# The mixer's output projection in matmuls of 256 columns instead of 512, on one core of a Trainium2

## The chip, the cores and the metric

The kernel runs on one core of a Trainium2 chip. The metric is the device time of one execution in microseconds, as the median of several runs. A core has a tensor engine (PE; its loads of stationary operands are listed on their own as PEld), a vector engine (DVE), a scalar engine (ACT), GpSimd (POOL), and a sync engine (SP) whose queue issues the DMA transfers here.

## The reference

Two layers over 256 tokens of width 1024 in float32. Each layer has three sub-layers, each with an RMS norm ahead of it and behind it:

```python
for l in range(DEPTH):
    h = _swiglu(_rmsnorm(x, g[0]), ffn_w_in[l, 0], ffn_w_out[l, 0])
    x = x + 0.5 * _rmsnorm(h, g[1])
    h = _mixer(_rmsnorm(x, g[2]), mix_w_in[l], mix_w_out[l], ...)
    x = x + _rmsnorm(h, g[3])
    h = _swiglu(_rmsnorm(x, g[4]), ffn_w_in[l, 1], ffn_w_out[l, 1])
    x = x + 0.5 * _rmsnorm(h, g[5])
```

The mixer projects the tokens to 3080 columns, runs four heads of differential attention and four heads of an mLSTM on them, and joins the two results of 512 columns each to `y`, 256 x 1024. Its last step is the output projection `y @ w_out` with a weight matrix of 1024 x 1024. This step is the one that is changed, once in each layer.

## The kernel before

The 256 tokens are two tiles of 128. A product with a weight matrix is made by `mm3` (lines 328 to 332) in three passes of float32r: each operand is split into a hi and a lo part, and hi*hi (L330), hi*lo (L331) and lo*hi (L332) add up in one PSUM bank of 128 x 512 float32. The transposed activations, 128 x 128, are the stationary operand, and the weights move, 512 columns to a matmul. The first two passes share the stationary operand `xh`, the third has `xl`.

The weights come in pieces of 1 MiB by a DMA on SP's queue (L265). ACT makes the hi part of a piece's half (`wh`, L280) and DVE the lo part (`wl`, L282). The tiles for these parts are few, so a cast often waits until PE has finished with an earlier piece.

The program's order is: feed-forward, mixer, feed-forward, for each of the two layers. In the mixer, `traverse` runs the input projection with the attention and the mLSTM between its products. Then comes the output projection (lines 615 to 638). It takes four pieces of weights and four banks `po[t][hf]` (named `bk` in the profile), one for each token tile t and half hf of the columns. `outp(t, part, hf)` makes four contraction steps k of three passes each into such a bank; part 0 is the attention's half of `y`, part 1 the mLSTM's. There are eight calls of `outp` in a layer, so 32 products or 96 matmuls. `outputs_ml` puts four transposes (L773) between them, and the next phase's `prenorm` eight transposes (L349). When a token tile's two banks are done, `postnorm` (lines 386 to 400) reads them: a square on ACT (L392) and a product on DVE (L395).

An order of instructions is set in two ways. From a phase's "ending" to the next feed-forward's "running" the order on PE is that of the program text, and this holds for the whole mixer. Elsewhere on PE, and on the other engines everywhere, a planner orders the instructions by readiness under its own costs, with a few turns given by hand (`after`).

Of the kernel before, what the change touches and what calls it, by code (L numbers as in the profile page):

```python
"""Two layers of macaron FFN / (diff attention | mLSTM) mixer / macaron FFN on one core.

Every product with a weight matrix runs as three float32r passes: an operand is
split exactly into hi (float32r, 12 significant bits) and lo = value - hi, and
hi*hi + hi*lo + lo*hi accumulate in one PSUM bank. The activations (transposed,
128 tokens a tile) are stationary and the weights move, 512 columns at a time.
"""
# [15 lines left out]
P = 128  # L23
# [26 lines left out]
def _pack(inp):  # L50
    """Lays the inputs out for the kernel, in the order in which it uses them."""
# [67 lines left out]
class _Trunk:  # L119
# [49 lines left out]
    def constants_mix(self):  # L169
# [26 lines left out]
        # lambda of both layers, on every partition  # L196
# [8 lines left out]
        # persistent tiles with fixed parts  # L205
# [25 lines left out]
    def after(self, ins, others):  # L231
        """ins takes its turn on its engine behind the others."""
        for o in others:
            self.tc.add_manual_dep(ins.ins, o.ins.name, mybir.DependencyInfo(
                mybir.DependencyClass.NoSync, mybir.DependencyReason.DATA), reason="turn")

    def table(self, name, last=None):
        """Loads a set of ScalarE's functions behind everything that uses another set."""
        self.loaded = self.nc.scalar.preload_act_table_set(name)
        self.after(self.loaded, self.users + ([last] if last else []))  # L240
        self.users = []

    def func(self, *args, **kw):
        """An activation that needs the set loaded last."""
        i = self.nc.scalar.activation(*args, **kw)  # L245
        self.after(i, [self.loaded])
        self.users.append(i)
        return i

    def piece(self):  # L250
        """The next 1 MiB of the weights as hi and lo: two times [P, 1024] each. While no
        mixer needs them, its 4 KiB buffers hold some of these."""
        parts = self.begin_piece()
        return [parts(), parts()]

    def begin_piece(self):
        """A function that gives a piece's halves one after the other."""
        nc, i = self.nc, self.piece_at
        self.piece_at += 1
        step = 1024  # L260
        if i in self.early:
            raw, step = self.early[i], 512
        else:
            raw = self.raw_tile(i)
            self.load = nc.sync.dma_start(raw.rearrange("p a b -> p (a b)"), self.a["w"][i])  # L265
        js = iter(range(2))

        def part():
            j = next(js)
            if self.lend and self.halves % 10 in (2, 5, 8):  # L270
                lo = self.k4.tile([P, 1024], F32R, tag="k4", name=f"wl_{i}_{j}")
                hi = self.k4.tile([P, 1024], F32R, tag="k4", name=f"wh_{i}_{j}")
            else:
                lo = self.wl.tile([P, 1024], F32R, tag="wl", name=f"wl_{i}_{j}")
                hi = self.wh.tile([P, 1024], F32R, tag="wh", name=f"wh_{i}_{j}")
            self.halves += 1
            turns = self.turns.pop(0) if self.turns else ()
            for c in range(0, 1024, step):
                cs = slice(c, c + step)
                ia = nc.scalar.activation(hi[:, cs], raw[:, j, cs], AF.Copy)  # L280
                self.cast = ia
                iv = nc.vector.tensor_tensor(lo[:, cs], raw[:, j, cs], hi[:, cs].bitcast(F32), op=ALU.subtract)  # L282
                for oa, ov in turns:
                    self.after(ia, [oa] if oa else [])
                    self.after(iv, [ov] if ov else [])
            return hi, lo

        return part
# [4 lines left out]
    def start(self):  # L293
        """The first loads, in the order in which the products need them."""
# [20 lines left out]
    def warm(self, n):  # L315
        """The tensor engine's clock rises while it waits for the first loads."""
        bank = self.bank_bk()
        for _ in range(n):
            self.nc.tensor.matmul(bank, self.zero[:, 0:P], self.zero, start=True, stop=True)

    @staticmethod
    def cols(piece, k):
        """Columns k*512..k*512+511 of a piece, hi and lo."""
# [4 lines left out]
    def mm3(self, ps, xh, xl, wh, wl, start, stop):  # L328
        mm = self.nc.tensor.matmul
        mm(ps, xh, wh, start=start, stop=False)  # L330
        mm(ps, xh, wl, start=False, stop=False)  # L331
        mm(ps, xl, wh, start=False, stop=stop)  # L332

# [1 line left out]
    def rsqrt(self, ss, width=1):  # L335
        """ss -> ss ** -0.5 on [P, width]."""
# [4 lines left out]
    def prenorm(self, t, gi):  # L341
        """Transposed x * gain of token tile t as hi/lo."""
        return [self.prenorm_half(t, gi, hf) for hf in range(2)]
# [19 lines left out]
    def square(self, t, hf, ss):  # L363
        """The mean square of half of token tile t."""
# [3 lines left out]
    def rstd(self, t):  # L368
        """rsqrt(mean(x ** 2) + eps) of token tile t."""
# [5 lines left out]
    def rsqrt_sum(self, ss, eps):  # L375
        """(ss0 + ss1 + eps) ** -0.5"""
# [9 lines left out]
    def postnorm(self, t, po, g, half):  # L386
        """x += (0.5 if half else 1) * rmsnorm(po) * g."""
# [83 lines left out]
    def ffn(self, pre, gi_post):  # L471
# [16 lines left out]
        if not xT:  # L488
            # the first phase: both token tiles from the start
# [41 lines left out]
        else:  # L531
            # the first two chunks: the first token tile runs ahead of the second
# [46 lines left out]
        # the last chunks: all of the first token tile, then the second  # L579
# [15 lines left out]
    def mixer(self, pre, gi_post):  # L595
# [19 lines left out]
        # output projection  # L615
# [4 lines left out]
        def outp(t, part, hf):  # L620
            for k in range(4):
                yh, yl = m.yT[t][part]
                self.mm3(po[t][hf], yh[:, k, :], yl[:, k, :], *self.cols(ws[2 * part + k // 2], 2 * (k % 2) + hf),
                         start=part == 0 and k == 0, stop=part == 1 and k == 3)
# [15 lines left out]
    def lambdas(self):  # L640
        """-(exp(q1.k1) - exp(q2.k2) + lambda_init) of both layers, on every partition."""
# [8 lines left out]
class _Mixer:  # L650
    """The stages of one layer's mixer, in the order in which they are traced."""
# [13 lines left out]
    def traverse(self, tr, pin, ws, pins1, ws1, load_gpost):  # L665
        """The rest of the input projection in steps of three matrix products, with everything
        else that the mixer does between them."""
# [53 lines left out]
    def stages(self):  # L721
        """(step, stage): the stage takes its turn once so many steps of the products are traced."""
# [37 lines left out]
    def part(self, t, kh, pin, w):  # L760
        """Half the contraction of one token tile with one group of 512 columns."""
# [7 lines left out]
    def transposed(self, a, tag="ptr"):  # L769
        """The four 128-column blocks of a, transposed, in a PSUM bank."""  # L770
# [12 lines left out]
    # ---- queries and keys of the mLSTM  # L783
# [31 lines left out]
    # ---- gates of the mLSTM  # L815
# [13 lines left out]
    def gate_inputs(self):  # L829
        """log i and the forget gate's input, tokens on partitions."""  # L830
# [24 lines left out]
    def gate_rows(self):  # L855
        """Cumulative log forget gates b, u = log i - b and the running maxima, heads on
        partitions 0..3, 32..35, 64..67 and 96..99."""
# [34 lines left out]
    def gate_exps(self, t):  # L892
        """exp(u_s - M_j) within a chunk and s <= j, zero elsewhere: one contraction over both."""
# [9 lines left out]
    def gate_decays(self):  # L903
        """The decays, input weights and exp(-m)."""
# [8 lines left out]
        # the first chunk's state is zero: its queries meet it with a factor of zero  # L913
# [5 lines left out]
    def weighted_qk(self):  # L919
        """Queries times their decay, keys times their input weight."""  # L920
# [24 lines left out]
    def intra_weights(self):  # L945
        """exp(u_s - M_j) * (k_s . q_j) / 8. Heads on other partitions use another PSUM bank."""
# [13 lines left out]
    # ---- attention  # L960
# [15 lines left out]
    def roped(self, i, t, scale):  # L976
        """Queries (i = 0) or keys (i = 1), transposed."""
# [10 lines left out]
    def scores(self, t, h0):  # L988
        """Both softmaxes of some heads before the division: exp(s - max) and its sums."""
# [29 lines left out]
    def combine(self, t, h0):  # L1019
        """l0 * (p0 - lambda * p1), transposed: [key, head, query]."""  # L1020
# [37 lines left out]
    # ---- state and output of the mLSTM; column 128 of a head's values is one, for the denominator  # L1058
# [36 lines left out]
    def output_gate(self, pin, t):  # L1095
        """tanh(o / 2): sigmoid(o) is half of it plus one."""
# [9 lines left out]
    def normed_ml(self, t):  # L1106
        """rmsnorm(num / max(|den|, exp(-m))) but for its gain: the norm takes the division's place."""
# [18 lines left out]
    def outputs_ml(self, t):  # L1126
        """sigmoid(o) times the normed output, transposed."""
# [37 lines left out]
```

## Time and profile before

| | |
|---|---|
| median of 3 runs | 1016.41 us (1015.97 to 1016.7) |
| span of the profiled execution | 1012.0 us |
| PE busy in it | 997.7 us (99%), 4701 matmuls, 4701 loads |
| DVE, ACT busy | 616.0 us (61%), 523.5 us (52%) |
| mean granted clock of PE | 0.997 |
| moved by DMA | 178.86 MB |

The span reaches from the first to the last instruction of the profiled execution; the timed runs also hold what lies around it. Busy time of PE is the union of its matmuls, each listed with its full latency, so matmuls in a row overlap; what one of them takes of the engine's time is read from the distance between two starts. Shapes are given as rows*columns of the stationary operand, then partitions x elements of the moving one. The type float32r is listed as f32 for PE.

### The profile page before, as it was taken

To read this page: it belongs to the slowest core of one execution; us is meant where nothing else is said; L and a number is where in the kernel's file an instruction comes from. 1 tells how busy PE (TensorE), PEld (TensorE's weight loads), DVE (VectorE), ACT (ScalarE), POOL (GpSimd) and SP (SyncE) were. 2 spreads that over 40 slices of the span, in tenths; PEclk is the share of its full clock that TensorE was granted. 3 is DMA by queue.
4 is the path that set the end of the run, shared out by engine and by line. 5 is a ranking of instruction groups with operands and counts; after the bars stand their busy time and mean duration, and the time that the engine had idled before them with its cause. 6 is when DMAs were issued, how large, how long until landed. Compare 5 with 4: busy or idle time off the path is not lost.

```text
span 1012.0 us, 12195 instructions
## 1 busy us (share of the span) xinstructions
PE 997.7 (99%) x4701; PEld 807.3 (80%) x4701; DVE 616.0 (61%) x867; ACT 523.5 (52%) x853; POOL 58.3 (6%) x60
## 2 busy tenths in 40 slices
PE   8999999999999999999999999999999999999997
PEld 5888888887788888888888888888877888888885
DVE  6755454589766755555485545456988586454542
ACT  6644444466755654444375544445768465444431
POOL 2000000014010000000000000001230100000000
PEclk9999999999999999999999999999999999999999
DMA  7954545335352745454346455543554247554511
GB/s 276 353 206 151 197 172 191 131 125 186 132 202 84 279 158 208 166 214 191 136 177 260 152 188 201 191 148 119 179 176 140 110 163 274 185 190 166 206 45 42
DMA packets 26809, 178.86 MB, mean 177 GB/s; under 512 B 2970, under 2 KB 3354, under 8 KB 6014
## 3 DMA queue, kind: packets, MB, share of 16 engines
q1 hardware_dynamic: 26750, 178.07, 48.4%
q8 instruction: 37, 0.61, 0.2%
q14 instruction: 22, 0.18, 0.1%
HBM read 177.01 MB, written 1.05 MB: 176 GB/s over the span
## 4 chain that ended last, share of the span: by engine, by line
PE 92%; DVE 5%; ACT 1%; DMA 1%; issue 0%; SPq 0%; DVEq 0%; POOLq 0%; ACTq 0%
PE pin L330 19%; PE pin L332 18%; PE pin L331 18%; PE bk L330 10%; PE bk L332 10%; PE bk L331 10%; PE ptr L461 2%; DVE wl L282 2%; DVE conv L806 1%; PE ptr L349 1%; PE ptr L773 1%; DMA wr<-in_w_dram 1%; ACT p L245 1%; PE bk L1086 1%; PE bk L1041 1%; ACT wh L280 0%
## 5 line engine op out<-in xcount | busy, mean ns | idle before, releaser
L282 DVE TENSOR_TENSOR wl<-wr,wh 128x1024 fp32r<-128x1024 f32 (+1 forms) x332 | 397.6, 1219 | 229.2 <-ACT wh L280 225.8
L280 ACT ACTIVATE wh<-wr 128x1024 fp32r<-128x1024 f32 (+1 forms) x332 | 340.4, 1045 | 203.5 <-PE pin L332 110.9
L330 PE MATMUL pin<-wh,th 128*128 128x512 f32 x880 | 350.7, 399 | 0.6 <-DVE rb L972 0.6
L332 PE MATMUL pin<-wh,tl 128*128 128x512 f32 x880 | 344.8, 392 | 0.0
L331 PE MATMUL pin<-wl,th 128*128 128x512 f32 x880 | 344.7, 392 | 0.0
L332 PEld LDWEIGHTS pin<-wh,tl 128*128 128x128 f32 x880 | 165.2, 188 | 36.4
L330 PEld LDWEIGHTS pin<-wh,th 128*128 128x128 f32 x880 | 165.3, 188 | 35.8 <-issue 1.0
L331 PEld LDWEIGHTS pin<-wl,th 128*128 128x128 f32 x880 | 165.5, 188 | 33.3
L330 PE MATMUL bk<-wh,hh 128*128 128x512 f32 x352 | 141.5, 402 | 0.0
L331 PE MATMUL bk<-wl,hh 128*128 128x512 f32 x352 | 139.6, 396 | 0.0
L332 PE MATMUL bk<-wh,hl 128*128 128x512 f32 x352 | 139.3, 397 | 0.0
L464 ACT ACTIVATE hh<-ptr 128x256 fp32r<-128x256 f32 x88 | 33.2, 378 | 101.2 <-PE ptr L461 83.3
L245 ACT ACTIVATE sil<-pin,rs 128x256 f32<-128x256 f32 x86 | 40.7, 473 | 75.3 <-PE pin L332 70.6
L332 PEld LDWEIGHTS bk<-wh,hl 128*128 128x128 f32 x352 | 66.2, 188 | 15.2
L331 PEld LDWEIGHTS bk<-wl,hh 128*128 128x128 f32 x352 | 66.2, 188 | 14.4
L330 PEld LDWEIGHTS bk<-wh,hh 128*128 128x128 f32 x352 | 66.2, 188 | 14.5
L465 DVE TENSOR_TENSOR hl<-ptr,hh 128x256 fp32r<-128x256 f32 x88 | 37.1, 422 | 59.2 <-ACT hh L464 56.3
L454 DVE SCALAR_TENSOR_TENSOR h<-pin,rs,sil 128x256 f32<-128x256 f32 x86 | 41.3, 480 | 31.9 <-ACT sil L245 31.9
L338 POOL TENSOR_TENSOR rs<-s,c_half 128x1 f32<-128x1 f32 x24 | 18.3, 766 | 623.1 <-DVE s L378 613.3
L461 PEld LDWEIGHTS ptr<-c,h 128*128 128x128 f32 x176 | 24.6, 140 | 11.9
L395 DVE TENSOR_TENSOR tmp<-bk,gpost 128x512 f32<-128x512 f32 x24 | 16.3, 689 | 29.3 <-ACT junk L392 29.3
L461 PE MATMUL ptr<-c,h 128*128 128x128 f32 x176 | 33.5, 272 | 0.0
(169 smaller groups left out, 617.0 us busy)
## 6 DMA issues: line engine op xcount, KB each, us to landing
wr<-in_w_dram SPq DMA_DIRECT2D x162, 1024.0 KB, 4.8
gpost<-in_gpost_dram SPq DMA_DIRECT2D x6, 512.0 KB, 6.4
wr<-in_w_dram SPq DMA_DIRECT2D x3, 512.0 KB, 8.9
x<-in_x_dram SPq DMA_DIRECT2D x4, 256.0 KB, 7.0
out_dram<-x SPq DMA_DIRECT2D x4, 256.0 KB, 2.0
wr<-in_w_dram SPq DMA_DIRECT2D x2, 256.0 KB, 4.6
lamv<-in_lam_dram SPq DMA_DIRECT2D x1, 256.0 KB, 3.2
c<-in_c_dram SPq DMA_DIRECT2D x1, 222.0 KB, 6.7
```

Source lines behind the costliest of these rows:

```text
L245: i = self.nc.scalar.activation(*args, **kw)
L280: ia = nc.scalar.activation(hi[:, cs], raw[:, j, cs], AF.Copy)
L282: iv = nc.vector.tensor_tensor(lo[:, cs], raw[:, j, cs], hi[:, cs].bitcast(F32), op=ALU.subtract)
L330: mm(ps, xh, wh, start=start, stop=False)
L331: mm(ps, xh, wl, start=False, stop=False)
L332: mm(ps, xl, wh, start=False, stop=stop)
L338: self.nc.gpsimd.tensor_tensor(r, ss, self.half[:, :width], op=ALU.pow)
L395: nc.vector.tensor_tensor(tmp[hf], po[hf], g[:, hf * 512:hf * 512 + 512], op=ALU.mult)
L454: nc.vector.scalar_tensor_tensor(h, pin[:, 256:512], r, sil, op0=ALU.mult, op1=ALU.mult)
L461: nc.tensor.transpose(ptr[:, k, :], h[:, k * P:(k + 1) * P], self.ident)
L464: nc.scalar.activation(hh, ptr, AF.Copy)
L465: nc.vector.tensor_tensor(hl, ptr, hh.bitcast(F32), op=ALU.subtract)
```

## The change

`mm3` passes further keywords on to the matmuls. In the mixer's output projection each product of 512 columns becomes two of 256 columns, into the first and the second half of the same bank. Each of the two makes its three passes with the same stationary operands. The flag that starts a bank's sum is set on the first half of the first product alone, and the flag that ends it on both halves of the last. The products of the feed-forward and of the mixer's input projection stay as they are. The rest of the diff only blanks comments and docstrings, and is left out here; the line numbers up to the output projection stay the same.

```diff
-    def mm3(self, ps, xh, xl, wh, wl, start, stop):
+    def mm3(self, ps, xh, xl, wh, wl, start, stop, **kw):
         mm = self.nc.tensor.matmul
-        mm(ps, xh, wh, start=start, stop=False)
-        mm(ps, xh, wl, start=False, stop=False)
-        mm(ps, xl, wh, start=False, stop=stop)
+        mm(ps, xh, wh, start=start, stop=False, **kw)
+        mm(ps, xh, wl, start=False, stop=False, **kw)
+        mm(ps, xl, wh, start=False, stop=stop, **kw)
...
         def outp(t, part, hf):
             for k in range(4):
                 yh, yl = m.yT[t][part]
-                self.mm3(po[t][hf], yh[:, k, :], yl[:, k, :], *self.cols(ws[2 * part + k // 2], 2 * (k % 2) + hf),
-                         start=part == 0 and k == 0, stop=part == 1 and k == 3)
+                wh, wl = self.cols(ws[2 * part + k // 2], 2 * (k % 2) + hf)
+                for n in range(2):
+                    c = slice(n * 256, n * 256 + 256)
+                    self.mm3(po[t][hf][:, c], yh[:, k, :], yl[:, k, :], wh[:, c], wl[:, c],
+                             start=part == 0 and k == 0 and n == 0, stop=part == 1 and k == 3, skip_group_check=True)
```

## Rows read from the trace of the kernel before

**Rows 1.** The page: busy time, granted clock by slice, chain that ended last.

```profile
PE 997.7 (99%) x4701; PEld 807.3 (80%) x4701; DVE 616.0 (61%) x867; ACT 523.5 (52%) x853; POOL 58.3 (6%) x60
...
PEclk9999999999999999999999999999999999999999
...
PE 92%; DVE 5%; ACT 1%; DMA 1%; issue 0%; SPq 0%; DVEq 0%; POOLq 0%; ACTq 0%
```

**Rows 2.** All waits of PE: total us, times, longest us.

```profile
PE bk L330 <- ACT th L358: 2.9, 1, 2.9
PE bk L924 <- DVE eh L917: 1.5, 2, 0.8
PE bk L319 <- DVE mp L875: 1.2, 1, 1.2
PE ptr L773 <- POOL ra L973: 0.9, 2, 0.5
PE pin L330 <- DVE rb L972: 0.6, 2, 0.3
PE bk L1088 <- DVE C L1074: 0.4, 2, 0.2
```

**Rows 3.** Windows on the two output projections; the columns stand in the first line.

```profile
core 0: us, PE busy (x) PEld busy (x) DVE busy (x) ACT busy (x) POOL busy (x), PEclk, DMA share, GB/s
295.50:319.00 23.50, 23.50 (x114) 19.35 (x112) 13.95 (x19) 9.48 (x16) 0.55 (x1) 1.00 0.37 135
...
792.00:816.50 24.50, 24.50 (x119) 20.32 (x118) 15.02 (x21) 9.96 (x17) 0.55 (x1) 1.00 0.37 129
```

**Rows 4.** Tiles yh and bk: count, min/median/max ns, first and last start us.

```profile
L330 PEld LDWEIGHTS bk<-wh,yh x64: 187/188/190, 295.5 to 815.7; 128*128 128x128 f32 x64
...
L331 PE MATMUL bk<-wl,yh x64: 387/389/398, 295.8 to 816.2; 128*128 128x512 f32 x64
...
L332 PE MATMUL bk<-wh,yl x64: 387/391/397, 296.1 to 816.4; 128*128 128x512 f32 x64
...
L1041 PE MATMUL bk<-vd,aT x48: 270/275/275, 282.1 to 781.9; 128*128 128x128 f32 x48
```

**Rows 5.** Timeline of PE in the first output projection: start us, duration us, instruction.

```profile
299.01 0.39 PE L331 MATMUL bk<-wl,yh 128*128 128x512 f32 x1
...
304.09 0.40 PE L332 MATMUL bk<-wh,yl 128*128 128x512 f32 x1
...
308.01 0.39 PE L332 MATMUL bk<-wh,yl 128*128 128x512 f32 x1
...
312.79 0.39 PE L332 MATMUL bk<-wh,yl 128*128 128x512 f32 x1
```

**Rows 6.** Timeline of PE and its loads behind a break, products of the mixer's input.

```profile
260.57 0.19 PEld L330 LDWEIGHTS pin<-wh,th 128*128 128x128 f32 x1
260.57 0.50 PE L330 MATMUL pin<-wh,th 128*128 128x512 f32 x1
260.68 0.19 PEld L331 LDWEIGHTS pin<-wl,th 128*128 128x128 f32 x1
...
260.91 0.39 PE L331 MATMUL pin<-wl,th 128*128 128x512 f32 x1
260.91 0.19 PEld L332 LDWEIGHTS pin<-wh,tl 128*128 128x128 f32 x1
```

**Rows 7.** Timelines: the second load and second matmul of L924's pair.

```profile
245.53 0.19 PEld L924 LDWEIGHTS bk<-eh,c_hotp 36*128 36x128 f32 x1
...
245.64 0.28 PE L924 MATMUL bk<-eh,c_hotp 36*128 36x256 f32 x1
```

**Rows 8.** Timeline of PE: first and last of 16 gate products in a row.

```profile
206.38 0.22 PE L822 MATMUL bk<-th,c_wgc 128*16 128x128 f32 x1
...
207.27 0.23 PE L823 MATMUL bk<-tl,c_wgc 128*16 128x128 f32 x1
```

**Rows 9.** Timeline of PE: the attention's 24 matmuls with the values, merged.

```profile
282.07 2.84 PE L1041 MATMUL bk<-vd,aT 128*128 128x128 f32 x24
```

**Rows 10.** Timeline of ACT and DVE where the first output projection ends.

```profile
316.39 1.04 ACT L280 ACTIVATE wh<-wr 128x1024 fp32r<-128x1024 f32 x1
...
317.47 1.23 DVE L282 TENSOR_TENSOR wl<-wr,wh 128x1024 fp32r<-128x1024 f32 x1 [0.25 <-ACT wh L280]
...
319.71 0.60 ACT L392 ACTIVATE junk<-bk 128x512 bf16<-128x512 f32 x1 [1.70 <-PE bk L332]
```

## What I expect, and why

> **What bounds the kernel now.** I read the page's first two parts, then the waits of PE, then the two stretches in which the change lies, and last the single instructions in them. The page [rows 1]: PE is busy 997.7 us of a span of 1012.0, its granted clock stands in the top tenth in every slice, and 92% of the chain that ended last lies on PE. The waits of PE [rows 2]: the longest is 2.9 us, for the first operand at the beginning, and the other five kinds come to 4.6 us in all, so no other engine holds PE up for more than a few us over the whole run. The stages [rows 3]: the first output projection starts at 295.5 us and the second has its last matmul at 816.4 [rows 4]; the two windows are theirs. In both PE is busy for the whole of the window (23.50 of 23.50, 24.50 of 24.50) at a granted clock of 1.00, its upper level of 2.4 GHz, while ACT is busy for 9.48 and DVE for 13.95 us of the first. So whatever PE needs more or less there reaches the end one for one, and what the other engines do there has room.
>
> Of the stage's products the trace has 64 of each of the three passes [rows 4]: 192 matmuls of 512 columns, and as many loads of the stationary operand, one for each matmul. The median of some 390 ns for a matmul is a latency and not its price, as the next one starts long before it ends; the price is the distance from start to start [rows 5]. From 299.01 to 304.09 us lie 22 steps, 230.9 ns each; from 308.01 to 312.79 us 21 steps, 227.6 ns each. I take the mean, 229.3 ns. At 2.4 GHz 512 columns alone are 213.3 ns, so 16.0 ns of each step are something else. The question of this change is whether those 16.0 ns belong to an instruction, and are then paid twice, or grow with the columns, and are then halved.
>
> **The change part by part.** *Removed:* 192 matmuls of 512 columns with 192 loads, at 229.3 ns: 44.03 us. *Added:* 384 matmuls of 256 columns with 384 loads. The same columns stream, the same sums are made in the same four banks. The order of the program puts the three passes of the first 256 columns ahead of the three of the second.
>
> The trace of before has no float32r matmul of 256 columns and 128 rows in a row of such, so its step is bounded from both sides.
>
> - The load. After a break, two loads stand 0.11 us apart (260.57 and 260.68), and the second matmul starts 0.23 us after its load [rows 6]: a load occupies its path for about 0.11 us. In steady running it starts with the matmul ahead of it (260.91 both), so 0.11 us of load lies under 0.23 us of streaming and costs nothing. With 256 columns (106.7 ns) the cover is just as long as the load. That is the point where the change could become dear, and the nearest row for it is L1041 [rows 9]: 24 matmuls with loads of the same 128x128 size within 2.84 us, the last one 0.275 us long as the median is [rows 4], so (2.84 - 0.275) / 23 = 111.5 ns a step. There too every load lies under only one such step, and a load that were not covered would add its own 0.11 us. So a load of this size can follow every 111.5 ns, and 111.5 ns is the lower bound.
> - The step from two sizes of the same type. The gate products L822 and L823 are float32r matmuls of 128 columns and 128 rows [rows 8]: 15 steps from 206.38 to 207.27 us, 59.3 ns each. A line through 59.3 ns at 128 and 229.3 ns at 512 columns rises by 0.4427 ns a column and gives 116.0 ns at 256. Their load is of 16 columns only, so this row says nothing of the cover; L1041 does.
> - A look at 256 columns itself: L924 is float32r with 256 columns, on 36 rows, and has two matmuls in a row [rows 7]. The second starts 0.11 us after its load (245.53, 245.64), where the 512 columns of [rows 6] needed 0.23. That agrees with half the price for half the columns.
> - The upper bound is that the whole 16.0 ns belong to the instruction: 106.7 + 16.0 = 122.7 ns.
>
> I take 116.0 ns, between the two rows of the same number type. The sum: 192 x (2 x 116.0 - 229.3) = 192 x 2.7 ns = +0.5 us. With the lower bound it is 192 x (2 x 111.5 - 229.3) = -1.2 us, with the upper one 192 x 16.1 = +3.1 us.
>
> The rule of the page "TensorE: Matmul & The Clock Gate" of the Trainium skill (section Back-to-back issue gap) is columns by 2.4 GHz and 2.5 ns for each matmul; by that the change would cost 192 x 2.5 ns = 0.5 us, an estimate from that page. The trace's own 229.3 ns differ from the 215.8 that the rule has for 512 columns, so the sum above goes by the rows.
>
> What waits on this: no wait is added. The first three matmuls of a product no longer finish the bank's second half, but the bank is read only after the last of its products, so ACT's square (L392) and the postnorm still wait for one last matmul. The lo half of a weight piece is let go one and a half steps later than before (0.1 us); ACT's casts wait on PE there (1.70 us of idle time ahead of L392, casts L280 of 1.04 us and DVE L282 of 1.23 us between, [rows 10]), and PE waits for none of them, so this costs nothing. No DMA is issued anew and none is moved on its queue. What follows the stage slides with it. PE's order within the mixer is written by hand; elsewhere, and on ACT and DVE everywhere, a planner sets it by its own costs, and it sees 384 matmuls in place of 192, so some instructions may change places.
>
> The profiled run's span of 1012.0 us is 4.4 us under the median of the timed runs, 1016.41; that part lies around the span and doesn't change. So 1016.41 + 0.5 = 1016.9 us.
>
> **The rivals.**
>
> - *The step has a fixed part* (slower). The 16.0 ns are paid once for each matmul, whatever its columns, on PE in the two stages: +3.1 us, 1019.5 us. For it: the step differs by 3.3 ns between two stretches with the same columns [rows 5], so a part of the 16.0 ns doesn't go with columns. Against it: the 128-column step has only 59.3 - 53.3 = 6.0 ns over its columns, and half of 512 columns is no dearer in [rows 7]. It decides from 119.9 ns a step on, where 192 x (2 x 119.9 - 229.3) passes 2.0 us.
> - *The floor is reached* (a small gain). The step is 111.5 ns as at L1041: -1.2 us, 1015.2 us, which can't be told from no change.
> - *The planner's order turns* after the first projection. One cast of a weight piece that falls behind the postnorm's work would hold PE by about 1.04 + 1.23 = 2.3 us [rows 10]: 1016.9 + 2.3 = 1019.2 us. It can also take away a wait; but all of PE's waits behind the first are 4.6 us together [rows 2], so a gain beyond 2 us is unlikely.
> - *The added loads are not covered.* Each added one would show as at a restart, 0.11 us (0.34 us from start to start at 260.57 in place of 0.23): 192 x 0.11 = +21 us, 1038 us. L1041 speaks against it. The same section of the Trainium skill also gives 81 ns for 128 and 131 ns for 512 columns in streams of load and matmul, from which a large fixed part would follow (64 ns a matmul, some +12 us, an estimate from that page); both the 59.3 and the 229.3 ns measured here contradict it.
> - *Loads are merged*, since two passes in a row share an operand: they do so before the change as well, and there is one load for each matmul [rows 4], so I give it nothing.
>
> **How the numbers follow.** Forecast 0.52, fixed part 0.18, floor 0.10, planner 0.18, loads not covered 0.02. About 0.2% (2.0 us) is what a measurement of this kernel can tell from no change: 1014.4 to 1018.4. Forecast and floor lie within it; the fixed part and the loads outside. Of the planner's 0.18 I put 0.10 above, 0.04 within and 0.04 below; and of the forecast's 0.52 I put 0.02 above, for a step near its upper bound, and 0.01 below. So faster 0.05, same 0.63, slower 0.32. The range runs from the floor, 1015.2, with 0.4 us for the spread of the runs (1015.97 to 1016.7), to the fixed part's 1019.5 with the same and a little of the planner's: 1014.8 to 1020.2.
>
> **What would show it.** In the profile of the changed kernel: 384 matmuls of 128x256 and 384 loads on the tiles bk<-w,y; steps of about 116 ns (111 to 113 would be the floor, 120 and more the fixed part, over 200 uncovered loads); PE busy throughout both stages. If these hold and the time still moves by more than 2 us, the planner's order did it, and then PE's waits list a new releaser. The forecast is wrong if the step is over 119.9 ns or PE's waits grow by more than 1.5 us.

## The result

The change costs 0.2%: in 16 runs each the median went from 1015.5 us to 1017.22 us, the ratio is 1.002 with a 95% interval of 1.0013 to 1.0026, so +1.3 to +2.6 us. The forecast was +0.5 us, 1016.9 us, and no measurable change; the range 1014.8 to 1020.2 us holds the time.

The profile of the changed kernel, as pages and views of the same kind as those of before. First the page: busy time, granted clock by slice, and the chain that ended last.

```profile
PE 999.7 (99%) x4893; PEld 817.6 (81%) x4893; DVE 615.8 (61%) x867; ACT 523.6 (52%) x853; POOL 58.4 (6%) x60
...
PEclk9999999999999999999999999999999999999999
...
PE 92%; DVE 5%; ACT 1%; DMA 1%; issue 0%; SPq 0%; DVEq 0%; POOLq 0%; ACTq 0%
```

There are 192 more matmuls and 192 more loads (4893 against 4701 in [rows 1]), PE's busy time is 2.0 us longer, and nothing else moved. The waits of PE are the six of [rows 2]; the first two of them:

```profile
PE bk L330 <- ACT th L358: 3.4, 1, 3.4
PE bk L927 <- DVE eh L920: 1.5, 2, 0.7
```

Only the first differs by more than 0.1 us, namely by 0.5; it lies in the first 10 us, where PE waits for the first operand that ACT makes (`th`). The order of the instructions on ACT, DVE, POOL and SP's queue is the same in both traces, and on PE it is the same outside the output projection. So the planner turned nothing.

The windows on the two output projections, with the columns of [rows 3]:

```profile
296.40:321.00 24.60, 24.60 (x210) 24.60 (x209) 14.25 (x19) 9.48 (x16) 0.55 (x1) 1.00 0.37 129
794.50:819.00 24.50, 24.50 (x210) 24.50 (x209) 14.26 (x19) 9.50 (x16) 0.55 (x1) 1.00 0.35 130
```

PE is busy throughout, as before. What is new stands in the third column: PEld is busy in 24.60 of 24.60 us, against 19.35 of 23.50 before. This does not yet say that the loads bind. A load is listed with some 187 ns, more than the distance between two steps, so the listed loads cover the stage as soon as the steps are that short. In the run with loads of half the size, told below, PEld is just as full, and the step is shorter:

```profile
296.00:320.00 24.00, 24.00 (x210) 24.00 (x209) 14.20 (x19) 9.43 (x16) 0.55 (x1) 1.00 0.36 132
```

Last the instructions of the changed kernel. The tile's own rows, with the columns of [rows 4]:

```profile
L331 PEld LDWEIGHTS bk<-wl,yh x128: 187/192/193, 296.5 to 818.8; 128*128 128x128 f32 x128
L331 PE MATMUL bk<-wl,yh x128: 277/283/283, 296.6 to 819.0; 128*128 128x256 f32 x128
```

And the timeline of PE with its loads, in one stretch, and then the first and the last matmul of the stage's last call of `outp`:

```profile
309.41 0.28 PE L332 MATMUL bk<-wh,yl 128*128 128x256 f32 x1
309.42 0.19 PEld L330 LDWEIGHTS bk<-wh,yh 128*128 128x128 f32 x1
309.53 0.28 PE L330 MATMUL bk<-wh,yh 128*128 128x256 f32 x1
309.54 0.19 PEld L331 LDWEIGHTS bk<-wl,yh 128*128 128x128 f32 x1
...
318.28 0.28 PE L330 MATMUL bk<-wh,yh 128*128 128x256 f32 x1
...
321.03 0.28 PE L332 MATMUL bk<-wh,yl 128*128 128x256 f32 x1
```

From 318.28 to 321.03 us lie 23 steps, 119.6 ns each. Over all 376 steps of the two stages that do not begin with the first matmul behind a transpose the mean is 119.1 ns, against 229.5 ns for the 184 such steps before. The eight steps that do take 202 ns in place of 317. The two stages together: 376 x 119.1 + 8 x 202 = 46.4 us, against 184 x 229.5 + 8 x 317 = 44.8 us, so +1.6 us. The distance from a stage's first matmul to the first one behind it says the same: 23.95 and 23.81 us before, 24.74 and 24.67 after, +0.79 and +0.86. Of the 2.6 us between the two spans (1014.6 and 1012.0) the other 0.9 lies in the first 10 us or so, ahead of everything that the edit touches, and two single runs can't say whether it comes again. The interval of the timed difference, +1.3 to +2.6 us, holds the stages' 1.6.

So the question left by the result: why is the step 119.1 ns and not 116.0, and is it a fixed part of a matmul, or the load?

### The profile page after: what moved, and what is told of

Its sections match the earlier page's. It is cut to its first block, busy times and chain, and to the rows that moved or that the text cites. A ratio compares the mean times of both kernels' runs of the same rounds, so it can differ in the third digit from the quotient of the medians.

```text
span 1014.6 us, 12579 instructions
## 1 busy us (share of the span) xinstructions
PE 999.7 (99%) x4893; PEld 817.6 (81%) x4893; DVE 615.8 (61%) x867; ACT 523.6 (52%) x853; POOL 58.4 (6%) x60
## 4 chain that ended last, share of the span: by engine, by line
PE 92%; DVE 5%; ACT 1%; DMA 1%; issue 0%; SPq 0%; DVEq 0%; POOLq 0%; ACTq 0%
PE pin L330 19%; PE pin L332 18%; PE pin L331 18%; PE bk L330 10%; PE bk L331 10%; PE bk L332 10%; PE ptr L461 2%; DVE wl L282 2%; DVE conv L809 1%; PE ptr L349 1%; DMA wr<-in_w_dram 1%; PE ptr L776 1%; ACT p L245 1%; PE bk L1089 1%; PE bk L1044 1%; ACT wh L280 0%
## 5 line engine op out<-in xcount | busy, mean ns | idle before, releaser
L282 DVE TENSOR_TENSOR wl<-wr,wh 128x1024 fp32r<-128x1024 f32 (+1 forms) x332 | 397.6, 1219 | 231.3 <-ACT wh L280 227.9
L330 PE MATMUL bk<-wh,yh 128*128 128x256 f32 x128 | 36.7, 287 | 0.0
L332 PE MATMUL bk<-wh,yl 128*128 128x256 f32 x128 | 36.2, 282 | 0.0
L331 PE MATMUL bk<-wl,yh 128*128 128x256 f32 x128 | 36.0, 282 | 0.0
```

Source lines behind the costliest of these rows:

```text
L330: mm(ps, xh, wh, start=start, stop=False, **kw)
L331: mm(ps, xh, wl, start=False, stop=False, **kw)
L332: mm(ps, xl, wh, start=False, stop=stop, **kw)
```

## Experiments: what a step consists of

The theories, as the expectations number them. 1: each matmul has a fixed part, 13.3 ns over its columns (106.7 + 13.3 = 120.0, the median step after). 2: the load sets the step. 3: adding twice in a row to the same columns of the bank holds PE up. 4: the fixed part belongs to the columns that are loaded. Later ones are named where they come up. All edits are on the changed kernel unless said otherwise.

**Four matmuls of 128 columns.**

```diff
-                for n in range(2):
-                    c = slice(n * 256, n * 256 + 256)
+                for n in range(4):
+                    c = slice(n * 128, n * 128 + 128)
```

> Each product of the two output projections as four matmuls of 128 columns, so 768 in place of 384. Theory 1, a fixed part: every float32r matmul with a load of 128 columns takes its columns at 2.4 GHz and 13.3 ns more (256 columns: 106.7 + 13.3 = 120.0 ns, which is the median step of the changed kernel). Then the step is 53.3 + 13.3 = 66.7 ns, and the two stages are 768 x 66.7 - 384 x 120.0 = 5 us longer together than in the changed kernel. Theory 2, the load sets the step: 120 ns is the load's own path (0.11 us) and a switch of operands, which 256 columns just fail to cover. Then the step stays at 110 to 120 ns, and the stages are 768 x 115 - 384 x 120.0 = 42 us longer.

One run: 1056.63 us, beside 1015.38 for the kernel before. The stages are 44.59 us each, 39.8 us more than in the changed kernel together; theory 2 expected 42, theory 1 expected 5. The timeline of PE in its first stage:

```profile
305.75 0.28 PE L330 MATMUL bk<-wh,yh 128*128 128x128 f32 x1
...
306.31 0.28 PE L332 MATMUL bk<-wh,yl 128*128 128x128 f32 x1
```

And the window on that stage:

```profile
296.90:341.50 44.60, 44.60 (x403) 44.60 (x402) 14.53 (x19) 9.71 (x16) 0.55 (x1) 1.00 0.20 72
```

Five steps in 0.56 us, 112 ns each (mean of all 768 steps: 112.0). A matmul of 128 columns is not cheaper than 112 ns when a stationary operand of 128x128 has to be loaded for it; the gate products of [rows 8], with loads of 16 columns, need 59.3. So a load of this size follows every 112 ns here and no faster, the 111.5 of L1041 [rows 9] is just this floor, and theory 1 falls as the whole story. But theory 2 doesn't explain the 119.1 ns either, as 112 is less than that.

**The passes in another order.**

```diff
-                for n in range(2):
-                    c = slice(n * 256, n * 256 + 256)
-                    self.mm3(po[t][hf][:, c], yh[:, k, :], yl[:, k, :], wh[:, c], wl[:, c],
-                             start=part == 0 and k == 0 and n == 0, stop=part == 1 and k == 3, skip_group_check=True)
+                for i, (x, v) in enumerate(((yh, wh), (yh, wl), (yl, wh))):
+                    for n in range(2):
+                        c = slice(n * 256, n * 256 + 256)
+                        self.nc.tensor.matmul(po[t][hf][:, c], x[:, k, :], v[:, c], start=part == 0 and k == 0 and i == 0 and n == 0,
+                                         stop=part == 1 and k == 3 and i == 2, skip_group_check=True)
```

> The changed kernel with the six matmuls of a product in another order: the first pass on both halves of the columns, then the second, then the third. Neighbouring matmuls go to different halves of the bank, and two to four in a row have the same stationary operand. Theories 1 (a fixed part of a matmul) and 2 (the load sets the step): nothing moves, the step stays at 120 ns, the stages within 0.3 us. Theory 3, adding twice in a row to the same 256 columns holds the matmul up: the step falls to about 107 to 110 ns, and the two stages together are 384 x 11 = 4 us shorter. If loads of an operand that is there already were left out, the count of loads would fall and theory 2 would have the step fall as well.

One run: 1016.09 us. The mean step is 119.2 ns, the stages are 24.77 and 24.66 us long; the loads are as many as the matmuls still (818.0 us of PEld, x4893). Theory 3 falls: with neighbours in different halves of the bank, and with two to four matmuls in a row on the same stationary operand, the step is the same.

**A narrower stationary operand.** The load is made smaller while 256 columns still move.

```diff
+                p = slice(0, P if part == 0 and k == 0 else 64)
...
-                    self.mm3(po[t][hf][:, c], yh[:, k, :], yl[:, k, :], wh[:, c], wl[:, c],
+                    self.mm3(po[t][hf][p, c], yh[:, k, p], yl[:, k, p], wh[:, c], wl[:, c],
```

> The changed kernel with a stationary operand of 64 columns in place of 128, in all contraction steps of the output projection but the first one; half of the tokens lack the products that are left out. 256 columns move in each matmul as before. Theory 1 (a fixed part of a matmul, whatever is loaded): the step stays at 120 ns. Theory 2 (the load sets the step): a load of half the size takes some 0.05 us and is covered, and the step falls to 107 to 112 ns. Theory 4, the 13.3 ns over the columns belong to the load's columns, though the load is covered: about 106.7 + 6.7 = 113 ns, where theory 2 and it can't be told apart by this run alone.

The mean step between two such matmuls is 115.1 ns, and most single steps lie between 113 and 120. Theory 1 asked for 120, theory 2 for 107 to 112, theory 4 for 113; none is met. To part theory 4 from the next one, the same edit was made with 32 and with 96 columns, after the runs with 384 and 512 columns told below:

> The changed kernel with a stationary operand of 32 columns in place of 128, in all contraction steps of the output projection but the first one; three quarters of the tokens lack the products that are left out. With 64 columns the mean step was 115.4 ns, with 128 it is 119.2. Theory 6: the streaming of 256 columns takes about 115.4 ns by itself, half of the 230 of 512, and only a load that is nearly as long (111.5 ns) adds to it; then the step stays at 115 to 116 ns. Theory 7, each loaded column adds its share (3.8 ns for 64 of them): 113.4 ns.

> As the run before it with 96 columns; a quarter of the tokens lack the products that are left out. Theory 6: a load of three quarters (some 0.08 us) is well covered by 115 ns, and the step is 115 to 116 ns. Theory 7: 115.4 + 1.9 = 117.3 ns.

The loads of 32, 64 and 96 columns, one kernel to a fence (rows by form: count, busy us, mean ns, idle us ahead of them):

```profile
L330 PEld LDWEIGHTS bk<-wh,yh 128*32 128x32 f32 x112 | 12.1, 108 | 0.8
```

```profile
L330 PEld LDWEIGHTS bk<-wh,yh 128*64 128x64 f32 x112 | 15.1, 134 | 0.0
```

```profile
L330 PEld LDWEIGHTS bk<-wh,yh 128*96 128x96 f32 x112 | 18.1, 161 | 0.0
```

And in the same order the first and the last matmul of the first stage's last call of `outp`, 23 steps apart, which answer to 318.28 and 321.03 above:

```profile
319.09 0.28 PE L330 MATMUL bk<-wh,yh 128*32 128x256 f32 x1
...
321.77 0.28 PE L332 MATMUL bk<-wh,yl 128*32 128x256 f32 x1
```

```profile
317.23 0.28 PE L330 MATMUL bk<-wh,yh 128*64 128x256 f32 x1
...
319.90 0.28 PE L332 MATMUL bk<-wh,yl 128*64 128x256 f32 x1
```

```profile
316.98 0.28 PE L330 MATMUL bk<-wh,yh 128*96 128x256 f32 x1
...
319.66 0.27 PE L332 MATMUL bk<-wh,yl 128*96 128x256 f32 x1
```

In these calls the steps are 116.5, 116.1 and 116.5 ns, with 128 columns 119.6. Over all steps of the two stages between two such matmuls: 115.7, 115.1, 116.8 and 119.1 ns for loads of 32, 64, 96 and 128 columns. The first contraction step in the same three runs keeps its full load, and its 44 steps in a run have means of 118.5 to 118.7 ns. So the step does not follow the load's size in proportion (theory 7: 113.4 at 32); it is flat at 115 to 116 ns, rises by about 1 ns at 96, and by 3.5 ns at 128. This is theory 6: 256 columns stream in about 115.5 ns, half of 512's, and a load adds to it when it is nearly as long. A narrower stationary operand also writes fewer partitions of the bank; that this makes the step shorter is ruled out by the run with 512 columns and a stationary operand of 64 below, where nothing gets shorter. The durations of the loads grow by (161 - 108) / 64 = 0.83 ns a column, 106 ns for 128. That is the rule of the Trainium skill's page "TensorE: Matmul & The Clock Gate" (section LDWEIGHTS (loading the stationary operand): columns by 1.2 GHz); the floor of 112 ns is a little above it.

**384 and 128 columns.**

```diff
-                for n in range(2):
-                    c = slice(n * 256, n * 256 + 256)
+                for n, c in enumerate((slice(0, 384), slice(384, 512))):
```

> Each product of the output projection as 384 and 128 columns. Theory 4 with the floor that the quarters showed: a step is the larger of 111.5 ns (the load's path) and columns at 2.4 GHz plus 13.3 ns. Then 384 columns take 160.0 + 13.3 = 173.3 ns, and 128 columns, whose own streaming and fixed part are 66.7 ns, wait for the load at 111.5 ns: 284.8 ns for the two against 240.0 with two of 256, 192 x 44.8 = +8.6 us on the two stages against the changed kernel. A fixed part alone, without the floor, gives 240.0 ns and no difference.

One run, 1028.2 us. A product is three matmuls of 384 columns and then three of 128. PE over two products, from the first matmul of one to that of the next but one:

```profile
312.10 0.39 PE L330 MATMUL bk<-wh,yh 128*128 128x384 f32 x1
312.32 0.34 PE L331 MATMUL bk<-wl,yh 128*128 128x384 f32 x1
312.50 0.34 PE L332 MATMUL bk<-wh,yl 128*128 128x384 f32 x1
312.67 0.22 PE L330 MATMUL bk<-wh,yh 128*128 128x128 f32 x1
312.73 0.27 PE L331 MATMUL bk<-wl,yh 128*128 128x128 f32 x1
312.85 0.27 PE L332 MATMUL bk<-wh,yl 128*128 128x128 f32 x1
312.96 0.40 PE L330 MATMUL bk<-wh,yh 128*128 128x384 f32 x1
...
313.82 0.39 PE L330 MATMUL bk<-wh,yh 128*128 128x384 f32 x1
```

A product takes 0.86 us, three times 287 ns (the same over the 48 products that stand in a row with others); 284.8 were expected with a floor, 240 without. The stages are 29.26 us each, +4.5 and +4.6 over the changed kernel: 9.1 us where 8.6 were expected. The means of a product's six steps are 229, 175 and 175 ns behind 384 columns and 60, 111 and 111 behind 128. The 60 of the first 128 and the 229 of the first 384 make 289 ns together, about a 175 and a 112, so it is the sum that counts. A load that finds too short a cover is paid for even where the neighbours have time to spare: 384 columns, at 175 ns, leave some 60 ns over a load's 112 unused, and the loads under the 128 still take 112 each. The run is 2 us longer than the stages explain. Some 1.6 us of it lie between the two stages, where the granted clock fell to its lower level, 1.2 GHz, for a few us (window of this run, columns as in [rows 3], and two matmuls in it):

```profile
781.00:783.90 2.90, 2.90 (x8) 2.23 (x8) 1.51 (x2) 2.37 (x8) 0.00 (x0) 0.50 0.89 311
```

```profile
781.65 0.63 PE L332 MATMUL pin<-wh,tl 128*128 128x512 f32 x1
782.08 0.63 PE L330 MATMUL pin<-wh,th 128*128 128x512 f32 x1
```

The work in the window is products of the mixer's input, 0.43 us from start to start in place of 0.23; ahead of it, from 776.0 to 780.6 us, PE had run the attention's and the mLSTM's small matmuls alone. The traces with 32 and 96 columns show one such fall too, at 277 and 774 us, behind the same work, and those of before and after none between their first 14 us and the end. So the time of a single run says nothing here about differences under 2 us.

**512 columns with a stationary operand of 64.** The edit is on the kernel before (left out: `mm3` passes the further keyword on, as in the change).

```diff
-                self.mm3(po[t][hf], yh[:, k, :], yl[:, k, :], *self.cols(ws[2 * part + k // 2], 2 * (k % 2) + hf),
-                         start=part == 0 and k == 0, stop=part == 1 and k == 3)
+                p = slice(0, P if part == 0 and k == 0 else 64)
+                self.mm3(po[t][hf][p], yh[:, k, p], yl[:, k, p], *self.cols(ws[2 * part + k // 2], 2 * (k % 2) + hf),
+                         start=part == 0 and k == 0, stop=part == 1 and k == 3, skip_group_check=True)
...
```

> The kernel before, 512 columns to a matmul, with a stationary operand of 64 columns in place of 128 in all contraction steps of the output projection but the first one; half of the tokens lack the products that are left out. Theory 4 (the fixed part belongs to the columns that are loaded, 0.104 ns each, covered or not): the calm step falls from 227 to 213.3 + 6.7 = 220 ns, and the two stages are some 168 x 6.7 = 1.1 us shorter together. If the part at 512 columns had another source than the one at 256, the step would stay at 227 to 232 ns.

The mean step is 230.3 ns, not lower than the 229.5 of before. Theory 4 falls for good: under 512 columns the load's size costs nothing. Nor does the width of the output: a gain for each matmul or for each column would show here as well.

**256 columns everywhere.**

```diff
         mm = self.nc.tensor.matmul
-        mm(ps, xh, wh, start=start, stop=False, **kw)
-        mm(ps, xh, wl, start=False, stop=False, **kw)
-        mm(ps, xl, wh, start=False, stop=stop, **kw)
+        kw["skip_group_check"] = True
+        for n in range(2):
+            c = slice(n * 256, n * 256 + 256)
+            mm(ps[:, c], xh, wh[:, c], start=start and n == 0, stop=False, **kw)
+            mm(ps[:, c], xh, wl[:, c], start=False, stop=False, **kw)
+            mm(ps[:, c], xl, wh[:, c], start=False, stop=stop, **kw)
...
```

`outp` calls `mm3` once for each product again, as in the kernel before; that part is left out.

> The same edit on all products that are made by the three passes: the feed-forward's and the mixer's input projection too, 3936 matmuls of 512 columns as 7872 of 256. Theories 1, 2 and 4: every step is 120 ns, so a product's pass takes 240 ns, against 227 to 233 ns now (mean 230.5): 3744 x 9.5 = +36 us over the changed kernel, if nothing but PE's own time changes, so about 1053 us. If the fixed part were what the sum of the prediction had, 2.7 ns a pass, it would be 3744 x 2.7 = +10 us, 1027 us.

1042.57 us (median of 4 runs), ratio to the kernel before 1.0267 (1.025 to 1.0285), so +27 us: the time lies between the two expected ones, 1053 and 1027 us. The page's line on busy time:

```profile
PE 1029.0 (99%) x8637; PEld 1016.3 (98%) x8637; DVE 617.4 (59%) x867; ACT 523.0 (50%) x853; POOL 58.6 (6%) x60
```

PE's busy time grows by 31.3 us over [rows 1], and PEld is now at 98%. The mean step is 119.3 ns for the input products (`pin`) and 119.2 for the feed-forward's second ones (`hh`), whatever their 512-column step was: 229.4 and 233.1 ns. The 36 us were too high in two places: 120.0 was taken for 119.3, and the `hh` products had less to lose, 2 x 119.2 - 233.1 = 5.3 ns a pass in place of 9.5. Of the 4 us between the 31.3 and the timed 27, 1.8 are idle time of PE that is gone: the span grows by 29.5 us only, from 1012.0 to 1041.5. The other 2.3 lie between the two profiled executions and the medians. PE's order in the feed-forward is the planner's and differs there, which was not followed up.

## A cause behind the 512-column step, and a faster kernel

The step at 512 columns has a mean of 227 ns in some calls of `outp` and of up to 233 in others (two stretches of them in [rows 5]), and of 233 for the `hh` products, while with 256 columns everywhere it lies near 119 (117 to 120 ns) wherever the tiles lie. Sorted by the place in SBUF that the program gives the tiles, the steps fall in two groups: where the moving operand and the next stationary one both begin at multiples of 256 bytes, the mean is 228.8 ns for the input products and 229.4 for the others, elsewhere it is mostly 231 to 234. The tiles `hh` and `hl` begin 160 bytes behind such a multiple, and four of the six buffers lent to the weight pieces 64 to 192 bytes, because two tiles, the mLSTM's values of 4128 bytes and the conv's padded input of 4144, have a size that is no multiple. Three versions of the kernel before move these places, and with them the tiles that lie behind; the instructions and their order on PE, ACT, DVE and POOL stay the same:

```diff
-        self.vx = self.ded.tile([P, NT, 4, P + 1], F32, name="vx")
+        self.vx = self.ded.tile([P, NT * 4 * (P + 1) + 24], F32, name="vx")[:, 0:NT * 4 * (P + 1)].rearrange(
+            "p (t h e) -> p t h e", t=NT, h=4)
```

> The kernel before, with one tile (the mLSTM's values) made 96 bytes longer, so that the feed-forward's stationary tiles hh and hl behind it begin at multiples of 128 bytes; before, they begin 32 bytes behind one. No instruction is added or moved. Theory 5: a load from 32 bytes behind a multiple of 64 costs the streaming matmul some 4 ns; the feed-forward's second product has a mean step of 233.1 ns, and the products of the same form with aligned stationary tiles 229.4. Then these 1056 steps fall to about 229 ns, and the kernel is 1056 x 4 = 4 us faster, some 1011 us. If the 233 ns have another cause (the bank, the order of the products), nothing moves.

The ratio is 0.9965 (0.9953 to 0.9978), 1012.35 us as the median of 5 runs: 3.6 us less, and the mean `hh` step falls from 233.1 to 230.1 ns (with an aligned moving operand to 229.3). In the second version the lent buffers are moved as well:

```diff
-            self.xpad = tr.t4("xpad", (P, 4, S + 3))
+            self.xpad = tr.t4("xpad", (P, 1056))[:, 0:4 * (S + 3)].rearrange("p (b s) -> p b s", b=4)
```

> As the run before it, and the conv's padded input made 80 bytes longer as well, so that the buffers which are lent to the weight pieces all begin at multiples of 128 bytes (before, two of them at multiples of 64 only). Theory 5 for the moving operand: steps from such a piece have a mean of 231.3 ns in place of 229.0, some 475 steps, so about 1 us more than the run before it gains, 5 us in all. If only the stationary tile's place matters, it equals the run before it.

The ratio is 0.9968 (0.9956 to 0.998), no better: the input products fall to 228.7 ns, but `hh`, which this version happens to put 128 bytes behind a multiple of 256, is at 232.1 again. A multiple of 128 is not enough. The third version has `+ 56` in the first edit and `(P, 1088)` in the second, and all places are multiples of 256:

> The kernel before, with two tiles made longer (the mLSTM's values by 224 bytes, the conv's padded input by 208) so that every stationary and every moving tile of the three-pass products begins at a multiple of 256 bytes. In the three runs with other places the mean step by place is: both at multiples of 256, 228.1 to 229.5 ns; one or both not, 231 to 233.6 ns. Theory 8: both places at multiples of 256 is what counts. Then all 3936 steps are at 228.5 ns on the mean instead of 230.4: 3936 x 1.9 = 7.5 us less, about 1008 us. If it is enough that the stationary tile lies well, it is as the run with that alone, 1012 us.

The ratio is 0.9908 (0.9895 to 0.9922), 1006.07 us as the median of 5 runs: 9.3 us less where theory 8 expected 7.5, the fastest version here. The mean step of all 512-column products is 227.8 ns in place of 230.4. Nine steps of `hh`, in the kernel before and in this version:

```profile
503.00 0.39 PE L332 MATMUL bk<-wh,hl 128*128 128x512 f32 x1
...
505.10 0.40 PE L332 MATMUL bk<-wh,hl 128*128 128x512 f32 x1
```

```profile
503.56 0.40 PE L333 MATMUL bk<-wh,hl 128*128 128x512 f32 x1
...
505.62 0.39 PE L333 MATMUL bk<-wh,hl 128*128 128x512 f32 x1
```

233.3 and 228.9 ns a step. The window from 30 to 200 us, 170 us of unbroken work, holds 764 matmuls before and 773 in this version:

```profile
30.00:200.00 170.00, 170.00 (x764) 138.11 (x763) 93.67 (x116) 79.94 (x111) 1.34 (x5) 1.00 0.55 198
```

```profile
30.00:200.00 170.00, 170.00 (x773) 139.87 (x772) 95.28 (x117) 82.20 (x114) 1.34 (x5) 1.00 0.56 202
```

Theory 8 is not the whole of it. The steps that were misplaced before fall by 4.9 ns (232.7 to 227.8, 1440 steps counted), but the steps whose two tiles lay at multiples of 256 already fall by 1.0 ns as well (228.9 to 227.9, 2216 steps), which is about a quarter of the gain. Why the place matters is not shown, and whether it is the operands' own place alone isn't either; shown is that moving the tiles shortens the steps.

## Why the prediction was right, and where it was off

- *What bounds the kernel, and that the stages' own time reaches the end:* right. The +1.6 us of the two stages is there at the end, and no other wait or order of an engine changed. One reading on the way was wrong: the 4.4 us between the span and the median of the timed runs do not all lie around the span. In each run whose span is on record the time is 1.7 to 1.8 us over it; so the profiled execution took some 1013.8 us, among the fastest of the 16 (1013.2 to 1016.7). The sum doesn't use the 4.4 us.
- *The time, 1016.9 us against 1017.22:* this closeness is luck. The forecast stood on three runs with a median of 1016.41; over 16 runs the kernel before has 1015.5. The base was 0.9 us too high and the step's term 1.2 us too low.
- *The price of 512 columns, 229.3 ns:* right, 229.5 over both stages. About 1 ns of it comes from the tiles' places (228.4 with all at multiples of 256).
- *The line through 59.3 and 229.3 ns, 116.0 at 256 columns:* right for the streaming, since with loads of 32 and 64 columns the step is 115.7 and 115.1 ns. There is no fixed part of 16 ns, the rival that came nearest: what was measured, +1.6 to +2.0 us, lies between the line's +0.5 and its +3.1, but not for its reason.
- *The load is covered and costs nothing:* this step failed. The text named the point itself, a cover just as long as the load, and took L1041's 111.5 ns as proof that a load is covered there. It proves only that loads can follow at that distance. 128 columns need some 59 ns by themselves [rows 8], so about half of each load stood uncovered at L1041: that row is the floor. Where the streaming (115.5) is 3.5 ns longer than the floor (112), a load of 128 columns still adds 3.5 ns a step. So the term is 192 x (2 x 119.1 - 229.5) = +1.7 us in place of +0.5, and the eight steps behind a transpose change next to nothing in it (202 + 119 ns against 317). Why loads and streaming of nearly the same length don't hide each other fully stays open; the runs show only the size.
- *The floor as a lower bound:* right as a bound. It decides from the point where a step's streaming is under 112 ns, as the quarters and the uneven split showed.
- *The planner, and loads merged or uncovered:* none of it came. The order was the same, and the loads stayed one to a matmul in each run.
- *The chances:* the change is at the edge of what can be told from none, and its interval, +1.3 to +2.6 us, lies on both sides of the 2.0 us that the prediction took as the border. So the runs don't decide between its "same" and its "slower". By its own sign, a step over 119.9 ns, the forecast stands by 0.8 ns only.

## What to carry to other kernels

A matmul's price is the distance of starts, and it has two parts to compare: its columns' streaming and the load that has to lie under the matmul ahead. Before columns are split, hold the load's own distance (112 ns here for 128 columns of float32r) against the shorter matmul's streaming. Where they were within 3% here, each matmul paid 3.5 ns; where the streaming was shorter, the load alone set the step. And a row of the trace that stands at the load's floor, as L1041 does here, shows how closely loads follow each other, not that a load is free under a matmul of nearly its length. Nor does a full PEld show that loads bind: the listed time of a load is longer than the step that it sets.

## What was not expected

Where the tiles lie in SBUF changes the step of a 512-column float32r matmul by 2 to 5 ns (227.8 to 229.4 with stationary and moving tile at multiples of 256 bytes, mostly 231 to 234 otherwise); over 3936 steps that is 9.3 us of 1015, about five times what the change under study moved, and it takes no more than a few padding bytes. And in three of the thirteen traces the granted clock falls to 1.2 GHz for a few us behind a stretch of the mixer's small matmuls; the input products under it then cost some 1.6 us more, as much as the change itself.
